# A hybrid decoder step on one Trainium2 core: token norms on two engines, another order for the compressed blocks, other buffers and queues for output weights

## The chip, the cores and the metric

The kernel runs on one core of one Trainium2 chip. The metric is the device time of one execution, in microseconds (us), as the median over several runs. TensorE (PE) multiplies; VectorE (DVE), ScalarE (ACT) and GpSimd (POOL) work element by element; SyncE (SP) issues most of the transfers from memory. Each engine works through its own queue in order.

## The reference, cut to what matters

One layer for a prompt of 1024 tokens and for 8 sequences of 4 new tokens (32 sample rows) with 1024 cached tokens each. `D` is 1024.

```python
h = rms_norm(x, g_pre)              # x * rsqrt(mean(x*x) + eps) * g_pre
u = h @ w_in                        # q, k/v and gates of two head groups, one matrix
# group 1 (8 heads): attention over compressed blocks, selected blocks and a window, mixed by gates
# compressed blocks: 32 rows at stride 16, + cmp_pos, @ w_cmp1, silu, @ w_cmp2, for keys and values,
#   of the prompt's own rows and of the cached rows of each of the 8 sequences
# group 2 (8 heads, "fox"): softmax attention with a forget gate
mix = concat(o_nsa * silu(z_nsa), o_fox * silu(z_fox))
x = x + rms_norm(mix @ w_out, g_post)
y = x + (p @ w_pproj) * sigmoid(x @ w_pgate)
```

## The kernel before

All is written in float32. A matrix product that has to be exact is made of three products of reduced float32 numbers: `split` (L80 to L86) writes a rounded high half on ScalarE and the rest as a low half on VectorE or GpSimd, and the matmuls take high by high, high by low, low by high. The author writes program order; a scheduler, which simulates all engines' timelines, orders each engine's queue from it, places tiles into the buffers of pools and sets all waits. A tile with `bufs=n` gets one of n buffers as soon as one is free; a pool that is opened where another was closed waits for that one's tiles.

**Stages.** First the token norm: nine tiles of x (eight of 128 prompt rows, one of 32 sample rows) are loaded on SP's queue, `sumsq` squares and sums them in two halves on ScalarE (L176), `rstd_of` (L97) makes the factors for four tiles at a time with small VectorE operations and one square root on ScalarE, VectorE and GpSimd scale the tiles (L204, L206), TensorE transposes them (L210), and `split` with the norm vector `gpre` as its scale writes the eight tiles `ht` (L85, L86), which hold the normalized prompt and sample rows transposed, as a high and a low half. `gpre` is loaded behind the x tiles.

Then the projections. `proj` (L227) loads 128 columns of `w_in` in four pieces `wr`, splits them into `wh` (ScalarE) and `wl` (GpSimd), and multiplies in three thirds of 352 columns, 24 matmuls each (L243). In the first part `cmp_proj(e)` makes the rows that are compressed (`cT`; e is 0 for keys, 1 for values). `cmp_pages` loads cached rows of two sequences (16 pieces on SP), and `cmp_chunk` transposes and splits these (L454, L462), multiplies with the compression weights (`w1`, L469) and stores the blocks; `cmp_chunk((NB,), None)` does it for the prompt's own rows from `cT`. `nsa_projections(1)` makes one projection for a later stage, and `gates_and_sums` is a generator whose `next` emits gate and forget sums in pieces. L535 to L578 give their order.

The middle (fox heads, sample attention, attention of group 1) is left alone by the change. At the end `weights` (L1285) loads `w_out` in eight pieces of 128 rows through two `stg` buffers and splits them into the 16 buffers `fwo`, the low halves in turn on VectorE and GpSimd; then, for each of eight prompt tiles, the mix and the gate z are loaded (into the same two `stg` buffers), multiplied, split, multiplied with `w_out` (`mm3`, L1305, 48 matmuls), and `tail` (L1333) norms, adds x and stores. After tile 1 all eight pieces of `w_pgate` are loaded on ScalarE's queue and split. The sample rows follow (`mm_s`, L1314), then the gated part.

Of the kernel before, what the change touches and what calls it, by code (L numbers as in the profile page):

```python
# [27 lines left out]
NB = 8  # L28
# [16 lines left out]
def tile_hymba_step(ctx: ExitStack, tc: tile.TileContext, I: dict, O: dict):  # L45
# [24 lines left out]

    cst = cpool.tile([128, C_ALL], F32, name="cst")
# [88 lines left out]
    HT = [hpool.tile([128, 2, TA], F32R, name=f"ht{k}", tag="ht") for k in range(KD)]  # L160
# [12 lines left out]
    def sumsq(ss, x, n):  # L173
        for c in range(2):
            jk = mm_tile("pt")
            nc.scalar.activation(jk[:n], x[:, c * 512:(c + 1) * 512], AF.Square, accum_out=ss[:, c])  # L176
# [12 lines left out]
    gpre = cpool.tile([128, KD], F32, name="gpre")  # L189
    nc.sync.dma_start(gpre, I["g_pre"][0].rearrange("(k p) -> p k", p=128))  # L190

    for g0 in (0, 4):
        ss = xpool.tile([128, 2, 4], F32, name="ss", bufs=2)
        rs = xpool.tile([128, 4], F32, name="rs", bufs=2)
        xts = []
        for t in range(4):
            xt = xta[g0 + t]
            sumsq(ss[:, :, t:t + 1], xt, 128)
            xts.append(xt)
        nc.vector.tensor_add(ss[:, 0], ss[:, 0], ss[:, 1])  # L200
        rstd_of(xpool, rs, ss[:, 0], 128)
        for t in range(4):
            if t % 2:
                nc.gpsimd.tensor_scalar(xts[t], xts[t], rs[:, t:t + 1], 0.0, op0=OP.mult, op1=OP.add)  # L204
            else:
                nc.vector.tensor_scalar(xts[t], xts[t], rs[:, t:t + 1], None, op0=OP.mult)  # L206
        for k in range(KD):
            ps = mm_tile(("fl", "sc")[k % 2])
# [4 lines left out]
    xs = xta[NT]  # L213
    ss1 = xpool.tile([NS, 2, 1], F32, name="ss1")
    rs1 = xpool.tile([NS, 1], F32, name="rs1")
    sumsq(ss1, xs, NS)
    nc.vector.tensor_add(ss1[:, 0], ss1[:, 0], ss1[:, 1])
    rstd_of(xpool, rs1, ss1[:, 0], NS)
    nc.vector.tensor_scalar(xs, xs, rs1, None, op0=OP.mult)
    ps = mm_tile()  # L220
    for k in range(KD):
        nc.tensor.transpose(ps[:, k * NS:(k + 1) * NS], xs[:, k * 128:(k + 1) * 128], ident[:NS, :NS])
    for k in range(KD):
        split(HT[k][:, 0, T:TA], HT[k][:, 1, T:TA], ps[:, k * NS:(k + 1) * NS], gpre[:, k:k + 1])
# [309 lines left out]

    pgs = cmp_pages((0, 1))  # L535
    cmp_proj(0)
# [18 lines left out]
    G = gates_and_sums()  # L555
    next(G)
    cmp_chunk((0, 1), pgs)
    nsa_projections(1)
    pgs = cmp_pages((2, 3))
    cmp_proj(1)  # L560
    cmp_chunk((2, 3), pgs)
    nsa_projections(1)
    pgs = cmp_pages((4, 5))
    next(G)
    nsa_projections(1)
    next(G)
    cmp_chunk((4, 5), pgs)
    nsa_projections(1)
    next(G)
    pgs = cmp_pages((6, 7))  # L570
    cmp_chunk((NB,), None)
# [713 lines left out]
    def weights(src, nk, pools, stage, q=nc.sync):  # L1285
        w = []
        for k in range(nk):
            wr = stage(k)
            q.dma_start(wr, src[k * 128:(k + 1) * 128])
            p, tag, bufs = pools[k]  # L1290
            h = p.tile([128, D], F32R, name="fwh", tag=tag, bufs=bufs)
            l = p.tile([128, D], F32R, name="fwl", tag=tag, bufs=bufs)
            split(h, l, wr, l_eng=(nc.vector, nc.gpsimd)[k % 2])
            w.append((h, l))
        return w

# [24 lines left out]
    wo = weights(w_out, 8, [(fr, "fwo", 16)] * 8, lambda k: stage())  # L1321
# [33 lines left out]
    nc.sync.dma_start(gpost, raw(I["g_post"], 0, [[0, 128], [1, D]]))  # L1355
    for t in range(NT):
        ts_ = slice(t * 128, (t + 1) * 128)
        mr = stage().rearrange("p (k c) -> p k c", c=128)
        nc.sync.dma_start(mr, d_mix[t // 4][:, :, t % 4 * 128:t % 4 * 128 + 128].rearrange("k p c -> p k c"))
        zr = stage().rearrange("p (k c) -> p k c", c=128)  # L1360
# [157 lines left out]
```

## Time and profile before

| | |
|---|---|
| median of 3 runs | 1294.2 us (1292.38 to 1298.24) |
| profiled execution, own time | 1289.5 us |
| its span, first to last instruction | 1287.7 us |
| mean granted clock of TensorE, 1 is 2.4 GHz | 0.978 |
| TensorE busy (matmuls) | 1194.4 us |
| VectorE / ScalarE / GpSimd busy | 670.0 / 604.1 / 312.8 us |
| read / written in HBM | 128.30 / 36.38 MB |

The profile is one execution; its times are microseconds from the span's start. A matmul's end is modelled, so the distance between two starts tells its pace. In brackets behind an instruction stands how long its engine had been idle before it, and what released it.

### The profile page before, as it was taken

How to read it: one execution, taken by the hardware profiler on the slowest of the kernel's cores; microseconds unless marked ns; L12 is line 12 of the kernel's file. 1: busy time of each engine (PE TensorE's matmuls, PEld its weight loads, DVE VectorE, ACT ScalarE, POOL GpSimd, SP SyncE). 2: the span in 40 equal slices, each digit the busy share in tenths (PEclk: the TensorE clock that was granted, in tenths of full speed). 3: DMA queues.
4: the chain of work that ended last, by engine and by line, in shares of the span. 5: the costliest groups of instructions: out<-in, count | busy, mean ns of one | idle time of the engine just before them, and what ended most of it. 6: DMA issues, size and time to landing. Idle time of an engine off the chain costs nothing. (4 is left out here: it accounts for less than half of the span.)

```text
span 1287.7 us, 23713 instructions
## 1 busy us (share of the span) xinstructions
PE 1194.4 (93%) x8106; PEld 981.2 (76%) x8106; DVE 670.0 (52%) x2062; ACT 604.1 (47%) x1415; POOL 312.8 (24%) x433
## 2 busy tenths in 40 slices
PE   3899989999999999999888899999999798999998
PEld 3798979989899898898865666564664576877776
DVE  4614455335655565553475677575455746443222
ACT  6724453244544555543465676574465742231121
POOL 2510100232222221312222232222112523131212
PEclk8999989999999999999988999999999998999999
DMA  7534311337321313224452543436645475532221
GB/s 243 137 93 136 83 48 49 96 90 227 90 55 48 106 53 95 68 76 149 136 159 95 161 132 127 153 124 223 193 138 174 140 240 171 165 139 82 71 74 38
DMA packets 142731, 157.04 MB, mean 122 GB/s; under 512 B 16586, under 2 KB 109546, under 8 KB 142418
## 3 DMA queue, kind: packets, MB, share of 16 engines
q1 hardware_dynamic: 141378, 151.06, 38.1%
q10 hardware_dynamic: 1152, 4.19, 0.9%
q8 instruction: 64, 1.05, 0.3%
q14 instruction: 57, 0.47, 0.1%
q0 software_dynamic: 80, 0.26, 0.1%
HBM read 128.30 MB, written 36.38 MB: 128 GB/s over the span
## 5 line engine op out<-in xcount | busy, mean ns | idle before, releaser
L243 PE MATMUL ps_fl<-ht,wh 128*128 128x352 f32 x1440 | 368.0, 329 | 5.6 <-DVE os L511 3.7
L243 PEld LDWEIGHTS ps_fl<-ht,wh 128*128 128x128 f32 x1440 | 256.6, 191 | 10.5 <-DVE os L511 4.0
L243 PE MATMUL ps_fl<-ht,wl 128*128 128x352 f32 x720 | 236.7, 329 | 0.0
L641 ACT ACTIVATE s<-s,m 128x64 f32<-128x64 f32 (+8 forms) x256 | 164.5, 644 | 59.6 <-DVE m L639 56.6
L83 POOL TENSOR_TENSOR wl<-wr,wh 128x256 fp32r<-128x256 f32 x120 | 89.1, 748 | 261.1 <-ACT wh L82 258.1
L644 POOL TENSOR_SCALAR s<-s,rs 128x64 f32<-128x64 f32 (+8 forms) x160 | 93.1, 601 | 234.6 <-DVE rs L1002 129.1
L243 PEld LDWEIGHTS ps_fl<-ht,wl 128*128 128x128 f32 x720 | 137.0, 190 | 1.1 <-issue 0.4
L633 PE MATMUL ps_sc<-kh,q 128*128 128x320 f32 (+12 forms) x304 | 117.3, 390 | 16.7 <-DVE m L639 10.7
L659 PE MATMUL ps_pt<-cst,s 128*128 128x128 f32 x816 | 127.0, 282 | 2.6 <-ACT s L93 1.0
L639 DVE CUSTOM_DVE_ANT_0 s<-ps_sc,bias 128x128 f32<-128x128 f32 (+10 forms) x224 | 80.4, 389 | 79.4 <-PE ps_pv L703 23.5
L659 PEld LDWEIGHTS ps_pt<-cst,s 128*128 128x128 f32 x816 | 97.1, 143 | 22.0 <-issue 5.6
L93 ACT ACTIVATE s<-ps_pt 128x512 f32<-128x512 f32 (+2 forms) x164 | 86.3, 538 | 56.3 <-PE ps_pt L659 44.6
L634 PE MATMUL ps_sc<-kl,q 128*128 128x320 f32 (+12 forms) x304 | 101.3, 336 | 1.5 <-DVE kl L622 1.5
L633 PEld LDWEIGHTS ps_sc<-kh,q 128*128 128x128 f32 x304 | 58.5, 192 | 50.5 <-DVE m L639 17.6
L639 DVE CUSTOM_DVE_ANT_0 s<-ps_sc,bias,m 128x320 f32<-128x320 f32 (+10 forms) x168 | 87.1, 523 | 7.0 <-PE ps_sc L634 3.4
L82 ACT CAST wh<-wr 128x256 fp32r<-128x256 f32 x120 | 47.7, 404 | 68.5 <-PE ps_fl L243 40.5
L95 DVE COPY s<-ps_pt 128x512 f32<-128x512 f32 (+2 forms) x84 | 49.8, 593 | 36.9 <-PE ps_pt L659 34.2
L769 POOL TENSOR_TENSOR mc<-bias,cst 128x128 f32<-128x128 f32 x64 | 30.2, 476 | 148.7 <-DVE m L639 134.7
L634 PEld LDWEIGHTS ps_sc<-kl,q 128*128 128x128 f32 x304 | 59.0, 194 | 3.7 <-DVE kl L622 1.7
L647 DVE TENSOR_SCALAR s<-s,rs 128x128 f32<-128x128 f32 (+7 forms) x96 | 54.5, 595 | 1.9
L1305 PE MATMUL ps_sc<-fwh,xh 128*128 128x512 f32 x128 | 50.8, 397 | 2.1 <-ACT xh L82 2.1
L1305 PE MATMUL ps_sc<-fwl,xh 128*128 128x512 f32 x128 | 50.1, 391 | 0.0
(444 smaller groups left out, 2191.1 us busy)
## 6 DMA issues: line engine op xcount, KB each, us to landing
kp<-in_cache_fox_kv_dram SPq DMA_DIRECT2D x64, 256.0 KB
vp<-in_cache_fox_kv_dram SPq DMA_DIRECT2D x64, 256.0 KB
wr<-in_w_in_dram SPq DMA_DIRECT2D x120, 128.0 KB
pg<-in_cache_cmp_kv_dram SPq DMA_DIRECT2D x64, 128.0 KB
pg<-in_cache_slc_kv_dram SPq DMA_DIRECT2D x64, 128.0 KB
d_g<-d_r SPq DMA_DIRECT2D x1, 4800.0 KB
bias<-d_g SPq DMA_DIRECT2D x8, 520.0 KB
X<-in_x_prompt_dram SPq DMA_DIRECT2D x8, 512.0 KB
```

The source lines that it names most:

```text
L83: (l_eng or nc.vector).tensor_tensor(l, src, h.bitcast(F32), op=OP.subtract)
L93: nc.scalar.activation(out, in_, AF.Copy, scale=1.0 if scale is None else scale)
L95: nc.vector.tensor_copy(out, in_)
L243: nc.tensor.matmul(ps[:, :CH], lhsT=w[k // 2][:, k % 2], rhs=HT[k][:, hl, s], start=n == 0, stop=n == 3 * KD - 1)
L633: nc.tensor.matmul(out, lhsT=qi, rhs=ks[0][:, k0:k0 + n], start=True, stop=False)
L634: nc.tensor.matmul(out, lhsT=qi, rhs=ks[1][:, k0:k0 + n], start=False, stop=True)
L639: nc.vector.tensor_tensor_reduce(o, p, bi, scale=-1.0, scalar=BIG if x == 0 else m, op0=OP.add, op1=OP.min, accum_out=m)
L641: nc.scalar.activation(s_ap, s_ap, AF.Exp, scale=-1.0, bias=m, accum_out=ssum)
L644: nc.gpsimd.tensor_scalar(s_ap, s_ap, r, 0.0, op0=OP.mult, op1=OP.add)
L647: nc.vector.tensor_scalar(s_ap, s_ap, r, None, op0=OP.mult)
L659: nc.tensor.transpose(ps[:, (2 * x + a) * 128:(2 * x + a + 1) * 128], S[:, a, (b0 + x) * 128:(b0 + x + 1) * 128], ident)
L1305: nc.tensor.matmul(o, lhsT=a[al][:, k], rhs=w[k][wl][:, c * 512:(c + 1) * 512], start=k == 0 and x == 0, stop=k == nk - 1 and x == 2)
```

## The change

`gpre` is loaded ahead of all else. The eight tiles `ht` become one tile of eight parts. The square of a whole tile is one instruction, on ScalarE for even and on VectorE for odd tiles, and writes its product into a part of the new tile that isn't in use yet; a square root of a constant stands ahead of them. The sample rows' factor is made with that of the second four tiles; the scaling is spread over three engines. The sample rows are multiplied by `gpre` and split in one piece. Both `cmp_proj` and the first `next(G)` go ahead of the pages and compression weights; the prompt's own chunk goes ahead of those of the sequences; and a projection stands ahead of every chunk. Six of the eight raw pieces of `w_out` are loaded into `fwo` buffers, the low halves of all these weights go to VectorE, z is loaded ahead of the mix, and the pieces of `w_pgate` come in pairs after tiles 1 to 4, on SP's queue.

```diff
--- before.py
+++ after.py
@@ -68,6 +68,8 @@
     def mm_tile(tag="fl"):
         return pst[1].tile([128, 512], F32, name="ps_" + tag, tag=tag, bufs=pst[2][tag])
 
+    gpre = cpool.tile([128, KD], F32, name="gpre")
+    nc.sync.dma_start(gpre, I["g_pre"][0].rearrange("(k p) -> p k", p=128))
     cst = cpool.tile([128, C_ALL], F32, name="cst")
     nc.sync.dma_start(cst, I["cst"])
     ident = cst[:, CO["ID"]]
@@ -157,7 +159,8 @@
     hpool = rst.enter_context(tc.tile_pool(name="hpool", bufs=8, side="right", reuse_waits="tile"))
     wpool = rst.enter_context(tc.tile_pool(name="wpool", bufs=3, side="right", reuse_waits="tile"))
 
-    HT = [hpool.tile([128, 2, TA], F32R, name=f"ht{k}", tag="ht") for k in range(KD)]
+    HA = hpool.tile([128, KD, 2, TA], F32R, name="ht", bufs=1)
+    HT = [HA[:, k] for k in range(KD)]
 
 
     qst = ExitStack()
@@ -170,10 +173,8 @@
     def xtile():
         return cp_.tile([128, 8 * XW], F32, name="X", tag="X", bufs=4)
 
-    def sumsq(ss, x, n):
-        for c in range(2):
-            jk = mm_tile("pt")
-            nc.scalar.activation(jk[:n], x[:, c * 512:(c + 1) * 512], AF.Square, accum_out=ss[:, c])
+    warm = cpool.tile([128, 1], F32, name="warm")
+    nc.scalar.activation(warm, ones[:, 0:1], AF.Sqrt)
 
     xta = []
     for t in range(NT + 1):
@@ -186,42 +187,56 @@
             xt = x2[:, (t % 2) * D:(t % 2 + 1) * D]
             nc.sync.dma_start(xt, x_p[t * 128:(t + 1) * 128, :])
         xta.append(xt)
-    gpre = cpool.tile([128, KD], F32, name="gpre")
-    nc.sync.dma_start(gpre, I["g_pre"][0].rearrange("(k p) -> p k", p=128))
-
+
+    def sumsq(ss, x, n, t):
+
+        jk = HA[:, 7 - t % 4].rearrange("p h c -> p (h c)")
+        if t % 2:
+            nc.vector.scalar_tensor_tensor(jk[:n, :D], x, 1.0, x, op0=OP.mult, op1=OP.mult, accum_out=ss)
+        else:
+            nc.scalar.activation(jk[:n, :D], x, AF.Square, accum_out=ss)
+
+    def scale(x, r, eng):
+        if eng == 0:
+            nc.vector.tensor_scalar(x, x, r, None, op0=OP.mult)
+        elif eng == 1:
+            nc.scalar.activation(x, x, AF.Identity, scale=r)
+        else:
+            nc.gpsimd.tensor_scalar(x, x, r, 0.0, op0=OP.mult, op1=OP.add)
+
+    rss = []
     for g0 in (0, 4):
-        ss = xpool.tile([128, 2, 4], F32, name="ss", bufs=2)
-        rs = xpool.tile([128, 4], F32, name="rs", bufs=2)
-        xts = []
+        ss = xpool.tile([128, 5], F32, name="ss", bufs=2)
+        rs = xpool.tile([128, 5], F32, name="rs", bufs=2)
+        rss.append(rs)
+        nc.gpsimd.memset(ss, float(D))
         for t in range(4):
-            xt = xta[g0 + t]
-            sumsq(ss[:, :, t:t + 1], xt, 128)
-            xts.append(xt)
-        nc.vector.tensor_add(ss[:, 0], ss[:, 0], ss[:, 1])
-        rstd_of(xpool, rs, ss[:, 0], 128)
-        for t in range(4):
-            if t % 2:
-                nc.gpsimd.tensor_scalar(xts[t], xts[t], rs[:, t:t + 1], 0.0, op0=OP.mult, op1=OP.add)
-            else:
-                nc.vector.tensor_scalar(xts[t], xts[t], rs[:, t:t + 1], None, op0=OP.mult)
+            sumsq(ss[:, t:t + 1], xta[g0 + t], 128, t)
+        if g0:
+            sumsq(ss[:NS, 4:5], xta[NT], NS, 0)
+        rstd_of(xpool, rs, ss, 128)
+        if g0 == 0:
+            for t in range(4):
+                scale(xta[t], rs[:, t:t + 1], t % 2)
+    for g0 in (0, 4):
+        xts = xta[g0:g0 + 4]
+        if g0:
+            for t in range(4):
+                scale(xts[t], rss[1][:, t:t + 1], (0, 2, 1, 2)[t])
+            scale(xta[NT], rss[1][:NS, 4:5], 0)
         for k in range(KD):
-            ps = mm_tile(("fl", "sc")[k % 2])
+            ps = mm_tile(("pt", "sc")[k % 2])
             for t in range(4):
                 nc.tensor.transpose(ps[:, t * 128:(t + 1) * 128], xts[t][:, k * 128:(k + 1) * 128], ident)
             s = slice(g0 * 128, g0 * 128 + 512)
             split(HT[k][:, 0, s], HT[k][:, 1, s], ps, gpre[:, k:k + 1])
-    xs = xta[NT]
-    ss1 = xpool.tile([NS, 2, 1], F32, name="ss1")
-    rs1 = xpool.tile([NS, 1], F32, name="rs1")
-    sumsq(ss1, xs, NS)
-    nc.vector.tensor_add(ss1[:, 0], ss1[:, 0], ss1[:, 1])
-    rstd_of(xpool, rs1, ss1[:, 0], NS)
-    nc.vector.tensor_scalar(xs, xs, rs1, None, op0=OP.mult)
     ps = mm_tile()
     for k in range(KD):
-        nc.tensor.transpose(ps[:, k * NS:(k + 1) * NS], xs[:, k * 128:(k + 1) * 128], ident[:NS, :NS])
-    for k in range(KD):
-        split(HT[k][:, 0, T:TA], HT[k][:, 1, T:TA], ps[:, k * NS:(k + 1) * NS], gpre[:, k:k + 1])
+        nc.tensor.transpose(ps[:, k * NS:(k + 1) * NS], xta[NT][:, k * 128:(k + 1) * 128], ident[:NS, :NS])
+    xsT = xpool.tile([128, KD, NS], F32, name="pc", tag="th", bufs=2)
+    nc.vector.tensor_tensor(xsT, ps[:, :KD * NS].rearrange("p (k c) -> p k c", c=NS),
+                            gpre[:, :, None].to_broadcast([128, KD, NS]), op=OP.mult)
+    split(HA[:, :, 0, T:TA], HA[:, :, 1, T:TA], xsT)
 
 
     def proj(c0, ev):
@@ -532,8 +547,11 @@
             f(c0, u)
         del nsa_out[:n]
 
+    cmp_proj(0)
+    cmp_proj(1)
+    G = gates_and_sums()
+    next(G)
     pgs = cmp_pages((0, 1))
-    cmp_proj(0)
     w1, w2, pos = [], [], []
     for e in range(2):
         w1h = cp_.tile([128, 16, 128], F32R, name="w1h", bufs=2)
@@ -552,23 +570,20 @@
         pT = cp_.tile([128, 16], F32, name="posT", bufs=2)
         nc.vector.tensor_copy(pT, ps[:, :16])
         pos.append(pT.rearrange("p (u j) -> p j u", u=2))
-    G = gates_and_sums()
+    nsa_projections(1)
+    cmp_chunk((NB,), None)
+    nsa_projections(1)
+    cmp_chunk((0, 1), pgs)
+    pgs = cmp_pages((2, 3))
     next(G)
-    cmp_chunk((0, 1), pgs)
     nsa_projections(1)
-    pgs = cmp_pages((2, 3))
-    cmp_proj(1)
     cmp_chunk((2, 3), pgs)
-    nsa_projections(1)
     pgs = cmp_pages((4, 5))
     next(G)
     nsa_projections(1)
+    cmp_chunk((4, 5), pgs)
+    pgs = cmp_pages((6, 7))
     next(G)
-    cmp_chunk((4, 5), pgs)
-    nsa_projections(1)
-    next(G)
-    pgs = cmp_pages((6, 7))
-    cmp_chunk((NB,), None)
     nsa_projections(1)
     next(G)
     cmp_chunk((6, 7), pgs)
@@ -1282,17 +1297,21 @@
     def stage_x(k):
         return fp.tile([128, 1280], F32, name="wx", tag=("xh", "xl")[k % 2], bufs=2)[:, :D]
 
-    def weights(src, nk, pools, stage, q=nc.sync):
+    def weights(src, ks, pools, stage):
         w = []
-        for k in range(nk):
+        for k in ks:
             wr = stage(k)
-            q.dma_start(wr, src[k * 128:(k + 1) * 128])
+            nc.sync.dma_start(wr, src[k * 128:(k + 1) * 128])
             p, tag, bufs = pools[k]
             h = p.tile([128, D], F32R, name="fwh", tag=tag, bufs=bufs)
             l = p.tile([128, D], F32R, name="fwl", tag=tag, bufs=bufs)
-            split(h, l, wr, l_eng=(nc.vector, nc.gpsimd)[k % 2])
+            split(h, l, wr)
             w.append((h, l))
         return w
+
+    def stage_o(k):
+
+        return fr.tile([128, D], F32, name="wro", tag="fwo", bufs=16) if k < 6 else stage()
 
     def halves(x):
         return [x[:, 0:512], x[:, 512:1024]]
@@ -1318,7 +1337,7 @@
             nc.scalar.copy(o, full[c][32:64])
             nc.vector.tensor_tensor(o, o, full[c][0:32], op=OP.add)
 
-    wo = weights(w_out, 8, [(fr, "fwo", 16)] * 8, lambda k: stage())
+    wo = weights(w_out, range(8), [(fr, "fwo", 16)] * 8, stage_o)
     ast.close()
     fpa = fst.enter_context(tc.tile_pool(name="fpa", bufs=1, reuse_waits="tile"))
     fp = fst.enter_context(tc.tile_pool(name="fp", bufs=1, reuse_waits="tile"))
@@ -1353,12 +1372,13 @@
 
     gpost = fr.tile([128, D], F32, name="gpost")
     nc.sync.dma_start(gpost, raw(I["g_post"], 0, [[0, 128], [1, D]]))
+    wg_ = []
     for t in range(NT):
         ts_ = slice(t * 128, (t + 1) * 128)
+        zr = stage().rearrange("p (k c) -> p k c", c=128)
+        nc.sync.dma_start(zr, d_z[:, :, ts_].rearrange("k p c -> p k c"))
         mr = stage().rearrange("p (k c) -> p k c", c=128)
         nc.sync.dma_start(mr, d_mix[t // 4][:, :, t % 4 * 128:t % 4 * 128 + 128].rearrange("k p c -> p k c"))
-        zr = stage().rearrange("p (k c) -> p k c", c=128)
-        nc.sync.dma_start(zr, d_z[:, :, ts_].rearrange("k p c -> p k c"))
         nc.vector.tensor_tensor(mr, mr, zr, op=OP.mult)
         mp = (fr, fp)[t % 2]
         mh = mp.tile([128, 8, 128], F32R, name="mh", tag="mh")
@@ -1369,8 +1389,8 @@
         o = [mm_tile(("fl", "sc")[t % 2]) for _ in range(2)]
         mm3(o, (mh, ml), wo, 8, (0, 1))
         tail(o, xr, 128, t)
-        if t == 1:
-            wg_ = weights(w_pgate, 8, [(fpa, "fwa", 8)] * 4 + [(fp, "fwb", 8)] * 4, stage_x, nc.scalar)
+        if 1 <= t <= 4:
+            wg_ += weights(w_pgate, (2 * t - 2, 2 * t - 1), [(fpa, "fwa", 8)] * 4 + [(fp, "fwb", 8)] * 4, stage_x)
     a_s = rows32(8)
     split(a_s[:, :8, 0:32], a_s[:, :8, 32:64], mixs)
     xr = row_tile()
@@ -1379,7 +1399,7 @@
     mm_s(o[:NS], a_s, wo, 8)
     tail(halves(o[:NS]), xr[:NS], NS, NT)
 
-    wp = weights(w_pproj, 2, [(fr, "fwo", 16)] * 2, lambda k: stage())
+    wp = weights(w_pproj, range(2), [(fr, "fwo", 16)] * 2, lambda k: stage())
 
     def gated(y, x1, n, g, pj):
```

## Rows read from the trace of the kernel before

**Rows 1.** The page, parts 1 and 2: busy time of all engines, TensorE's slices.
```profile
PE 1194.4 (93%) x8106; PEld 981.2 (76%) x8106; DVE 670.0 (52%) x2062; ACT 604.1 (47%) x1415; POOL 312.8 (24%) x433
...
PE   3899989999999999999888899999999798999998
```

**Rows 2.** Busy time by window: start:end, length, each engine, PEclk, DMA share, GB/s.
```profile
20.00:40.00 20.00, 14.24 (x77) 10.39 (x75) 17.28 (x35) 15.43 (x31) 9.78 (x11) 0.81 0.63 160
```

**Rows 3.** Timeline of SP's queue (start, us, engine, line, op, tiles), first 30 us.
```profile
7.94 0.39 SPq L190 DMA_DIRECT2D gpre<-in_g_pre_dram  x1
11.42 14.92 SPq L148 DMA_DIRECT2D pg<-in_cache_cmp_kv_dram  x16
26.39 1.61 SPq L231 DMA_DIRECT2D wr<-in_w_in_dram  x3
28.04 1.72 SPq L543 DMA_DIRECT2D w1r<-in_w_cmp_dram  x2
```

**Rows 4.** Timeline of TensorE, first projection and some page transposes.
```profile
40.19 0.63 PE L243 MATMUL ps_fl<-ht,wh 128*128 128x352 f32 x1 [0.33 <-DVE ht L86]
...
49.91 1.04 PE L454 MATMUL ps_sc<-cst,pg 128*128 128x128 f32 x8
...
54.32 0.32 PE L243 MATMUL ps_fl<-ht,wl 128*128 128x352 f32 x1
54.48 0.32 PE L243 MATMUL ps_fl<-ht,wh 128*128 128x352 f32 x1
```

**Rows 5.** Groups by line, 0 to 330 us: busy us, mean ns | idle before.
```profile
L82 ACT CAST X<-cT 64x512 fp32r<-64x512 f32 x8 | 8.6, 1071 | 0.1
L83 DVE TENSOR_TENSOR X<-cT,X 64x512 fp32r<-64x512 f32 x8 | 8.2, 1022 | 1.1 <-ACT X L82 0.7
L86 DVE SCALAR_TENSOR_TENSOR ht<-ps_sc,gpre,ht 128x512 fp32r<-128x512 f32 x8 | 5.9, 743 | 2.1 <-ACT ht L85 2.1
...
L204 POOL TENSOR_SCALAR X<-X,rs 128x1024 f32<-128x1024 f32 x4 | 5.3, 1344 | 19.9 <-DVE rs L106 15.2 <-ACT ht L85 4.7
```

**Rows 6.** Timeline of VectorE, 10 to 17 us.
```profile
12.12 0.17 DVE L100 TENSOR_SCALAR rs_v<-ss 128x4 f32<-128x4 f32 x1
...
14.68 0.16 DVE L103 TENSOR_TENSOR rs_a<-rs 128x4 f32<-128x4 f32 x1 [2.17 <-ACT rs L102]
...
15.47 2.29 DVE L206 TENSOR_SCALAR X<-X,rs 128x1024 f32<-128x1024 f32 x2
```

**Rows 7.** Busy time by window around 170 us, columns as in rows 2.
```profile
160.00:180.00 20.00, 14.04 (x89) 12.82 (x88) 15.56 (x39) 13.73 (x20) 2.85 (x4) 0.81 0.27 71
175.00:180.00 5.00, 4.68 (x23) 3.75 (x23) 4.20 (x13) 1.24 (x3) 2.22 (x4) 0.50 0.59 161
180.00:185.00 5.00, 5.00 (x29) 5.00 (x28) 0.55 (x2) 0.00 (x0) 0.00 (x0) 0.74 0.10 24
```

**Rows 8.** Timelines of VectorE, GpSimd and TensorE, last attention tile.
```profile
1027.95 1.59 DVE L1000 TENSOR_SCALAR rs<-sums 128x6 f32<-128x6 f32 x1 [1.20 <-ACT s L641]
...
1027.17 2.34 POOL L83 TENSOR_TENSOR fwl<-stg,fwh 128x1024 fp32r<-128x1024 f32 x1 [5.89 <-ACT fwh L82]
...
1032.26 0.33 PE L686 MATMUL ps_pt<-cst,s 128*128 128x128 f32 x1 [4.71 <-POOL s L644]
```

**Rows 9.** Timelines of TensorE, VectorE and GpSimd after the second output tile.
```profile
1063.71 0.39 PE L1305 MATMUL ps_sc<-fwl,mh 128*128 128x512 f32 x1
1063.94 0.40 PE L1305 MATMUL ps_sc<-fwh,ml 128*128 128x512 f32 x1
1070.70 0.79 PE L1314 MATMUL ps_pv<-fwh,as 128*128 128x512 f32 x1 [6.37 <-DVE as L83]
...
1077.34 0.39 PE L1305 MATMUL ps_fl<-fwh,mh 128*128 128x512 f32 x1
...
1068.03 2.29 DVE L106 TENSOR_TENSOR r<-r,rs_a 128x1 f32<-128x1 f32 x1
...
1064.67 5.62 POOL L83 TENSOR_TENSOR fwl<-wx,fwh 128x1024 fp32r<-128x1024 f32 x2 [5.70 <-ACT fwh L82]
```

## What was predicted

> **What bounds the kernel now.** I read the page's first two parts first [rows 1]. TensorE's matmuls are busy for 93% of the span, VectorE for 52%, ScalarE for 47%. The forty slices show where the other 7% lies: in the first two slices, the sixth, four from the twentieth on (attention, which the change leaves alone), the thirty-second, the thirty-fourth and the last. Since TensorE is nearly full elsewhere, whatever starts its stream earlier or closes a gap should move the end by as much. So I looked at the gaps alone, in order of time: the instructions of TensorE and of the other engines around each of them, the queue of SP, and windows of some microseconds.
>
> The front. In the stretch from 20 to 40 us TensorE shows 14.24 us of transposes at a granted clock of 0.81, VectorE 17.28 and ScalarE 15.43 [rows 2]: here the vector engines set the pace. The first projection matmul starts at 40.19, the last of that projection at 54.48 [rows 4]; the matmuls follow each other 0.16 us apart when nothing is in the way. Three things stand ahead of it. The factors of the first four token tiles come late: the chain stands still for 2.17 us between reciprocal and square root, behind the squares and a table load in ScalarE's queue, and scaling begins at 15.47 [rows 6]. The page loads of the first two sequences hold SP's queue from 11.42 for 14.92 us, so the first projection weights are issued at 26.39 [rows 3]. And the splits of those pages are mixed among the 16 splits of the normalized prompt, which cost VectorE 743 ns each [rows 5].
>
> The second gap is in the window from 160 to 180: TensorE has 14.04 us busy of 20, and afterwards runs five microseconds at the lower level, 1.2 GHz (granted clock 0.50), and then at a mean of 0.74 [rows 7]. What fills ScalarE and VectorE there is the compression of the prompt itself, 8 casts of 1071 ns and 8 subtractions of 1022 ns [rows 5].
>
> The third is at the end of attention. TensorE waits 4.71 us, until 1032.26, for GpSimd's scaling; the reciprocal chain ahead of that began with an operation over 6 columns that took 1.59 us, while GpSimd computed a low half of the output weights, from 1027.17 for 2.34 us [rows 8]. An operation of the same kind over 4 columns took 0.17 us [rows 6]. The fourth: the second output tile ends at about 1064.2, then nothing for 6.37 us, then the sample rows' 16 matmuls until 1077.34 [rows 9]. VectorE was late there: a multiplication of one column took 2.29 us, beside two low halves of gate weights on GpSimd that took 5.62 us in all [rows 9]. The third output tile needs the PSUM that the first tile's norm, queued on VectorE, still holds.
>
> **The change part by part.** *Norm.* Squares: 8 tiles on ScalarE become 4 there and 4 on VectorE; the square root's table is loaded at the start. That removes the 2.17 us stall and some waiting behind squares, so I let scaling start at 14.0 instead of 15.47 (the first four tiles still have to be loaded). The norm vector's transfer moves ahead of everything on SP: its issue takes 0.39 us [rows 3] and delays the tiles by about that; I take 0.5 (bounds 0.4 and 1.5). From 14.0 VectorE has: four scalings at 1.15 (2.29 for two [rows 6]), 4.6; two squares, at twice the 743 ns of half as wide an operation [rows 5], an estimate, 3.0; six small operations at 0.17 [rows 6], 1.0; 16 splits at 0.743, 11.9. Together 20.5, so all of the prompt is split at about 34.5. The sample rows, once 8 pairs of small splits, are one pair.
>
> *Order.* Both compressed projections, then the gate loads, then the pages. The projection weights thus go out behind the prompt, past the 16 page loads, and are there before 20 us. The first third of a projection needs only the first half of the prompt and runs while the second half is split. The second third ends as the splits do, and the last third is 24 matmuls at 0.16, 3.9 us. So the first projection ends near 39 instead of 54.6: 15.6 us. By then TensorE had also done the 32 page transposes of the first chunk, which now come later; 8 take 1.04 us [rows 4], so 4.2 go off. Front: 11 us. Lower bound 4 (a wait for the whole normalized tile, below), upper 14 (scalings at half that price, and part of the second projection fitted in).
>
> What becomes late: pages and the compression weights. They are loaded in pieces through two buffers, the first from 28.04 on [rows 3], and are now wanted at about 39 plus two projections of 11.5 (72 matmuls at 0.16), so there is room. GpSimd's queue has the projection weights' low halves and two scalings of 1344 ns [rows 5] beside these, and nothing of it is on the path unless they come late.
>
> *Prompt's blocks first, a projection per chunk.* The 8.6 and 8.2 us of splits [rows 5] now stand beside two whole projections of 11.5 us each, and each chunk's page splits beside one. The gap is 6.0 us of idle time (20 less 14.04). The clock cost half of 4.68 us, 2.3, and a quarter of 5, 1.3 [rows 7]: 9.6 in all. The order of the queues is new, and small waits will come up; I take 8 (bounds 3 and 9.6).
>
> *Output weights.* Six raw tiles get buffers of their own, so loads no longer wait for the splits two tiles back, and the low halves leave GpSimd for VectorE. The 1.59 us operation should fall to 0.17: 1.4 us gained. Against it, VectorE gets four more subtractions, in a stretch where it is fairly full; cost unknown, between nothing (in its gaps) and 5.9 us (an estimate: four times twice the 743 ns of an operation half as wide [rows 5]); I take 1, nearer to nothing, since the weights are wanted only after attention.
>
> *Gate weights.* Eight loads after tile 1 become two after each of tiles 1 to 4, on SP's queue, all halves on VectorE. GpSimd no longer holds VectorE up, and a tile has 11 us of matmuls (48 at 0.23) for two splits. I expect the third tile straight behind the second: 6.4 us of idle time. The sample's 16 matmuls, 6.64 us from 1070.70 to 1077.34 [rows 9], would be 16 times the 0.23 us between two starts before the gap [rows 9], 3.7: 2.9 more. Together 9.3, I take 9 (bounds 2, and 13, if tile 0's matmuls also fill part of the 4.71 us wait). Behind a waiting weight load on SP would stand the next tile's inputs and the stores of this one.
>
> Sum: 11 + 8 + 1.4 + 9, less 0.5 and 1: 28 us. The profiled execution took 1289.5 us, its span 1287.7; less 28 that is 1261.5. The median of the runs lies 4.7 above the profiled one, so 1266.
>
> One rule speaks against the front. The Trainium skill, "SBUF — State Buffer", section "Who interferes with whom", says that VectorE and GpSimd share a port pair, so that a VectorE operation with two SBUF inputs, or in a two-port mode, and a GpSimd operation that reads SBUF exclude each other for a whole instruction. The new squares on VectorE have two SBUF inputs. By the rule each of GpSimd's two scalings could hold VectorE up in full, and the sum would be 25 instead of 28; the 1.15 us scalings that I used already hold part of that.
>
> **The rivals.**
> (1) *Whole-tile wait.* The eight normalized tiles become one. If a projection waits for the whole of it, its first matmul starts at 34.5 and it ends at 46.0: the front gives 4 instead of 11, 1273. For it: the trace can't show such a tile. Against: in this kernel token tiles already share one buffer by halves and are scaled one by one.
> (2) *The first stage is held by its feeders.* The compression weights come behind 16 page loads that take SP 14.92 us [rows 3]. If the prompt's chunk finds them some 13 us late, TensorE waits at its head, and the two gains of 19 shrink to 6: 1279.
> (3) *The gap after tile 1 stays.* The tail's small operations may still queue behind a split that waits for its load. Then the 9 are gone: 1275.
> (4) *Port exclusion in full*, as computed from rows: two GpSimd scalings of 1.34 us: 3 us less, 1269.
> (5) *Slower.* On SP's queue a weight load that waits for a staging buffer stops the inputs of the next tile. If each of the four tiles then shows a gap like the old one, 9.3 us, that is 37 in place of 9.3, on top of the front's gain: 28 - 9 - 28 = -9, so 1303. It decides from some 7 us in each of four tiles on. Against it: a tile lasts 11 us, and a weight piece is only 512 KB, as much as one token tile.
>
> **How the numbers follow.** The forecast has 0.55, rivals (1) 0.12, (2) 0.13, (3) 0.08, (4) 0.06, (5) 0.06. The predicted time is the forecast's, 1266. The range has to take in (1) to (4) with some overlap among them, and on the low side the upper bounds of front and gate weights (14 and 13 instead of 11 and 9, with all of the second gap): 1254 to 1283. Under 0.5%, 6.5 us, a measurement can't tell a difference; faster means under 1287.7. Two of the rivals at once come near that line, and (5) lies beyond: faster 0.87, same 0.06, slower 0.07.
>
> **What would show it.** Right: first projection matmul near 20 us, end of that projection near 39; no window of 5 us between 40 and 230 with TensorE under 4 us busy; the stage's last instructions about 19 us earlier than before; no gap between the second and third output tile; no VectorE operation of a few columns over 1 us near the end of attention. Wrong: a first projection matmul after 30 us; a wait of TensorE for compression weights; SP waiting between two output tiles; a longer attention part, which the sum takes as unchanged.

## The result and the profile after

The kernel after takes 1302.7 us (median of 7 runs, 1301.13 to 1306.79) beside 1294.2 for the kernel before (7 runs, 1287.41 to 1298.24): ratio 1.0076, 95% interval 1.0051 to 1.01. It is slower by 0.8%; 1266 was predicted, with a chance of 0.07 for slower. The profiled execution took 1301.71 us, its span 1299.9, 12.2 longer than before.

The first reading is where TensorE comes later. These are starts of its instructions in the two timelines, in us:

| place | before | after | difference |
|---|---|---|---|
| first projection matmul | 40.19 | 35.05 | -5.1 |
| end of the first stage (first matmul with the compressed values `vcp`) | 234.7 | 249.8 | +15.1 |
| first output matmul | 1041.90 | 1058.15 | +16.2 |
| first product of the gated part | 1150.1 | 1162.7 | +12.6 |

So the first stage, from which 19 us were to come, lost 15, though its first projection starts 5 earlier; the end won some 4, and attention between them lost 1. TensorE has the same work, 1195.5 us beside 1194.4, in a longer span.

The windows (columns as in [rows 2]) place it. From 20 to 40 TensorE has 10.15 us busy where it had 14.24, at a mean clock of 0.66; the losses go on to 100. The gap of [rows 7] is nearly closed: 18.71 of 20. First the kernel after, then three windows of the kernel before:

```profile
20.00:40.00 20.00, 10.15 (x52) 8.37 (x50) 11.53 (x20) 10.13 (x21) 12.56 (x12) 0.66 0.40 109
40.00:60.00 20.00, 15.47 (x100) 14.43 (x98) 10.66 (x16) 14.46 (x24) 7.88 (x8) 0.88 0.32 90
60.00:80.00 20.00, 14.88 (x85) 14.02 (x84) 5.87 (x10) 7.57 (x13) 2.93 (x4) 0.84 0.26 67
80.00:100.00 20.00, 16.92 (x92) 15.27 (x91) 7.50 (x18) 8.20 (x15) 0.00 (x0) 0.76 0.43 126
160.00:180.00 20.00, 18.71 (x126) 18.33 (x127) 13.02 (x40) 10.44 (x20) 0.00 (x0) 0.91 0.38 105
```

```profile
40.00:60.00 20.00, 18.54 (x115) 17.52 (x116) 11.87 (x26) 14.69 (x35) 10.09 (x10) 0.93 0.45 123
60.00:80.00 20.00, 19.92 (x146) 19.02 (x145) 3.56 (x18) 4.03 (x9) 0.00 (x0) 1.00 0.42 122
80.00:100.00 20.00, 18.95 (x126) 18.50 (x125) 5.48 (x10) 8.98 (x19) 5.89 (x8) 1.00 0.30 84
```

TensorE's timeline names the waits:

```profile
30.11 1.12 PE L230 MATMUL ps_pt<-cst,X 128*128 128x128 f32 x4 [6.60 <-DVE ht L88]
...
35.05 0.66 PE L258 MATMUL ps_fl<-ht,wh 128*128 128x352 f32 x1
...
57.50 0.64 PE L277 MATMUL ps_fl<-cst,cT 128*32 128x128 f32 x2 [4.14 <-ACT nat L95]
...
75.11 0.23 PE L569 MATMUL ps_fl<-cst,pn 16*128 16x16 f32 x1 [1.70 <-DVE sn L278]
78.63 0.58 PE L489 MATMUL ps_pv<-X,w1h 128*128 128x260 f32 x1 [3.29 <-DVE X L85]
```

Each is followed to its head on another engine. The 6.60 end with a split of `ht` on VectorE, which waited for ScalarE, which waited for a transfer. ScalarE's timeline and SP's queue (the one of [rows 3]):

```profile
27.21 0.62 ACT L84 CAST w1h<-w1r 128x512 fp32r<-128x512 f32 x1 [5.29 <-DMA w1r<-in_w_cmp_dram]
27.74 0.20 ACT L104 ACTIVATE rs<-rs_a 128x5 f32<-128x5 f32 x1
27.84 0.67 ACT L87 ACTIVATE ht<-ps_pt,gpre 128x512 fp32r<-128x512 f32 x1
```

```profile
16.00 2.93 SPq L285 DMA_DIRECT2D bf<-in_b_fgate_dram  x1
24.45 0.92 SPq L561 DMA_DIRECT2D w1r<-in_w_cmp_dram  x2
...
78.27 8.95 SPq L150 DMA_DIRECT2D pg<-in_cache_cmp_kv_dram  x14
```

The cast of the first compression weights stands in ScalarE's queue ahead of the second half's square root and of 14 splits, and those weights are issued only at 24.45. From 18.93 to 24.45 SP shows no transfer: in its instruction list stand there the readings of 16 page numbers, two sequences of eight, into registers (L146), called by `cmp_pages`, which program order has ahead of the weights. The pages themselves go out from 72.7 on, since their buffers are still taken. (The expectations of e5 and e9 below speak of 32 numbers; the list has 16.)

VectorE (as in [rows 6]): the stall before the square root's result fell from 2.17 to 0.90 us, but tiles came later and a square of 1.22 us went between the factor's small operations, so scaling starts at 16.17, not 14.0. The last split of `ht` is at 49.58, not 34.5, and the first projection ends near 51.9, not 39.

```profile
14.34 0.17 DVE L105 TENSOR_TENSOR rs_a<-rs 128x5 f32<-128x5 f32 x1 [0.90 <-ACT rs L104]
14.42 1.22 DVE L195 SCALAR_TENSOR_TENSOR ht<-X 128x1024 fp32r<-128x1024 f32 x1
...
16.17 1.42 DVE L201 TENSOR_SCALAR X<-X,rs 128x1024 f32<-128x1024 f32 x2
...
49.58 0.75 DVE L88 SCALAR_TENSOR_TENSOR ht<-ps_sc,gpre,ht 128x512 fp32r<-128x512 f32 x1 [1.59 <-ACT ht L87]
```

At the end (timelines of VectorE, GpSimd and TensorE, as in [rows 8, 9]) the slow operation over 6 columns is down from 1.59 to 0.17 us as forecast, yet TensorE's wait for GpSimd grew from 4.71 to 7.33. The gap ahead of the sample rows is 3.21 instead of 6.37.

```profile
1044.22 0.17 DVE L1015 TENSOR_SCALAR rs<-sums 128x6 f32<-128x6 f32 x1
...
1045.00 5.66 POOL L659 TENSOR_SCALAR s<-s,rs 128x64 f32<-128x64 f32 x5 [11.26 <-DVE rs L1017]
...
1040.63 0.39 PE L718 MATMUL ps_pv<-s,vcz 128*64 128x128 f32 x4
1040.95 0.41 PE L648 MATMUL ps_sc<-kh,q 128*128 128x320 f32 x1
1041.20 0.31 PE L649 MATMUL ps_sc<-kl,q 128*128 128x320 f32 x1
1048.85 0.48 PE L701 MATMUL ps_pt<-cst,s 128*128 128x128 f32 x1 [7.33 <-POOL s L659]
...
1083.72 0.79 PE L1333 MATMUL ps_pv<-fwh,as 128*128 128x512 f32 x1 [3.21 <-DVE as L85]
```

Before, the second of the last pair of score matmuls stood at 1024.27, ahead of 3 us of weighted sums; now the pair stands behind them. The kernel before:

```profile
1024.27 0.31 PE L634 MATMUL ps_sc<-kl,q 128*128 128x320 f32 x1
1024.51 1.08 PE L697 MATMUL ps_pv<-s,VW 128*64 128x256 f32 x8
...
1027.15 0.39 PE L703 MATMUL ps_pv<-s,vcz 128*64 128x128 f32 x4
```

From that matmul to the one that needs the scaled result it took 8.0 us before (to 1032.26 [rows 8]) and 7.7 after. GpSimd's five scalings in it became slower, 5.66 us instead of 3.70, but the distance as a whole did not grow: the wait is longer because the 3 us of cover are gone.

### The profile page after: what moved, and what is told of

Same layout as the page of the kernel before. It is cut to its first block, busy times and chain, and to the rows that moved or that the text cites. A ratio compares the mean times of both kernels' runs of the same rounds, so it can differ in the third digit from the quotient of the medians.

```text
span 1299.9 us, 23670 instructions
## 1 busy us (share of the span) xinstructions
PE 1195.5 (92%) x8106; PEld 984.8 (76%) x8106; DVE 674.9 (52%) x2063; ACT 599.8 (46%) x1384; POOL 293.0 (23%) x424
## 5 line engine op out<-in xcount | busy, mean ns | idle before, releaser
L258 PEld LDWEIGHTS ps_fl<-ht,wh 128*128 128x128 f32 x1440 | 259.2, 193 | 8.6 <-DVE os L526 4.1
L659 POOL TENSOR_SCALAR s<-s,rs 128x64 f32<-128x64 f32 (+8 forms) x160 | 96.5, 624 | 250.8 <-DVE rs L1017 132.8
```

Of the source, the lines that this page charges most:

```text
L258: nc.tensor.matmul(ps[:, :CH], lhsT=w[k // 2][:, k % 2], rhs=HT[k][:, hl, s], start=n == 0, stop=n == 3 * KD - 1)
L659: nc.gpsimd.tensor_scalar(s_ap, s_ap, r, 0.0, op0=OP.mult, op1=OP.add)
```

## The experiments

Ratios are to the kernel before on the same chip, with their 95% intervals.

### Which part loses

e1, e2, e3 and e4 are made by putting whole parts of the diff on the kernel before: the norm; the order; both; the end. No code is new.

Norm alone. 

> The kernel before with the norm part alone (factors first, squares and scalings on two engines, one tile for the normalized prompt, the norm vector loaded first). Theory: the first stage was lost by the new order of its queues, not by the norm, so this one takes about 1292 (1288 to 1296), and the stage's last matmuls end within 4 us of the 234.7 of before. Rival: the norm itself costs (tiles land 1.2 us later, one tile for all): 1300 or more, the stage's end at 242 or later.

Measured: 1290.78 us, 0.9989 (0.9967 to 1.0012); the first stage ends at 233.5. As the theory had it.

Order alone. 

> The kernel before with the order part alone (both compressed projections, gate loads, then pages; prompt's blocks first; a projection per chunk). Theory: here lies the loss, about 15 us: 1309 (1303 to 1314), the stage's end near 250. Rival, the norm is to blame: within 4 us of 1294. Second rival, only both together lose: within 4 us of 1294 here and in the run with the norm alone.

Measured: 1308.61 us, 1.0134 (1.01 to 1.0168); the stage ends at 245.3, and TensorE has the same kind of wait as in after, 6.16 us until 31.52. The order is the loss, without any help of the norm.

Both, without the end. 

> The kernel after with the end of before: norm and order changed, output and gate weights as they were. Theory: the end part won some 4 us, so this is 4 slower than after: 1307 (1304 to 1310). Rival, the end is worth nothing (its gain at the gap eaten by the longer wait for GpSimd): 1303.

Measured: 1305.44 us, 1.0106 (1.0075 to 1.0138); the stage ends at 249.3. Between this and after lie 0.3%, which the intervals don't separate from nothing.

The end alone. 

> The kernel before with the end part alone (raw output weights in their ring, gate weights in pairs, all low halves on VectorE). Theory: 4 us faster, 1290 (1287 to 1292): the gap ahead of the sample rows' matmuls falls from 6.4 to some 3 us, the wait for GpSimd after the last attention tile grows from 4.7 to some 7. Rival, no gain: 1294. Second rival, the forecast's 9 us come once the first stage no longer shifts the attention part: 1285.

Measured: 1291.99 us, 0.9989 (0.9964 to 1.0014): no gain that the runs can tell from none, where the theory had 4 us. The wait for GpSimd is 7.33 us again, the gap 3.8 instead of 6.4: one pays for the other.

### What in the order loses

The page numbers:

```diff
 cmp_proj(0); cmp_proj(1); G = gates_and_sums(); next(G)
-pgs = cmp_pages((0, 1))
 w1, w2, pos = [], [], []
 for e in range(2):
     ...
     pos.append(pT.rearrange("p (u j) -> p j u", u=2))
+pgs = cmp_pages((0, 1))
```

> The kernel after, with the page loads of the first two sequences called behind the block of compression weights instead of ahead of it; on SP's queue the 32 page numbers are then read (18.9 to 24.4 us in after) behind the first compression weights. Theory: these weights are issued near 19 instead of 24.45 and land near 22, ScalarE no longer stands 5.29 us before their cast with the second half's square root and splits behind it, the first projection matmul comes near 30 instead of 35.05: some 5 us, and up to 2 more of clock: 1297 (1295 to 1299). Rival: another wait at the same place takes over (the fourth piece of the projection weights is now behind the page numbers): 1302.

Measured: 1294.79 us, 1.0004 (0.9979 to 1.0028), so 0.7% below after, a little more than the theory said. ScalarE's wait before the weights' cast is 0.78 us, and the first projection matmul comes at 29.5. The rival has a part: SP issues nothing from 21.4 to 27.0, where the numbers are now read, and the wait for the next piece of projection weights is new:

```profile
22.58 0.62 ACT L84 CAST w1h<-w1r 128x512 fp32r<-128x512 f32 x1 [0.78 <-DMA w1r<-in_w_cmp_dram]
...
29.27 0.40 ACT L84 CAST wh<-wr 128x256 fp32r<-128x256 f32 x1 [4.31 <-DMA wr<-in_w_in_dram]
```

The position tables (`cmp_pos`, 16 columns each):

```diff
+pos = []
+for e in range(2):
+    pn = ...; nc.sync.dma_start(pn, ...); transpose; copy; pos.append(...)
 cmp_proj(0)
 cmp_proj(1)
 ...
-    pn = ...        # the same lines, behind the compression weights
```

> The kernel after, with the two small position tables loaded, transposed and copied ahead of the compressed projections instead of behind the compression weights. Theory: ahead of the prompt's blocks TensorE waits 1.70 and 3.29 us for a 16-column table that stands on VectorE and ScalarE behind the 8.5 us split of the second projection; with the table there the blocks start near 73.5 instead of 78.6, and at a higher clock: 5 to 7 us, 1297 (1295 to 1299). Rival: the page loads (landing up to 88 us) then bound this stretch, and the gain is under 2 us: 1301.

Measured: 1293.17 us, 0.9998 (0.9971 to 1.0024), 0.8% below after. The waits of 1.70 and 3.29 us are gone and the prompt's blocks start at 72.0 instead of 78.6, more than the theory said. The wait at 30 us stays (5.3).

> Both of the former edits in one kernel. Theory: two separate waits, so the gains add up: 1291 (1288 to 1294), near the kernel before. Rival: what one closes the other opens again: 1297, no better than the better of the two.

Measured: 1289.89 us, 0.9956 (0.9942 to 0.997). After lies at 1.0076; the two edits alone took 0.0072 and 0.0078 off, together 0.0120. So they add up for the most part, and two small blocks put elsewhere undo the whole loss. (The end part, still in this kernel, has no share in it that the runs show: e4.)

The prompt's blocks last, as before (`cmp_chunk((NB,), None)` put straight ahead of the last chunk of pages, all else as in after; in the kernel before a projection and a `next(G)` stood between the two). 

> The kernel after, with the prompt's compressed blocks in their former place, before the last chunk of pages, and everything else as it is in after. Theory: the loss lies at the queues' heads in the first 90 us, and without the prompt's blocks there the first chunk of pages, loaded from 72.7 on, is waited for instead: 1303 to 1308. Rival: taking the prompt's blocks first is the loss: 1294 or less.

Measured: 1309.09 us, 1.0122 (1.0075 to 1.0169). So the prompt's blocks in front are not the loss. The waits of TensorE in the first 252 us (total, times, longest) show what comes with this order: the late pages, and for `os`, at 203 us, a wait of the kind that ended the old gap of [rows 7]:

```profile
PE ps_pt L230 <- DVE ht L88: 7.7, 2, 6.1
PE ps_sc L469 <- DMA pg<-in_cache_cmp_kv_dram: 7.2, 6, 4.2
PE ps_fl L258 <- DVE os L526: 5.9, 1, 5.9
```

The page numbers behind the last load of compression weights on SP:

```diff
+if hold and len(page_dmas) < 16:       # hold: the last w1r load
+    with tc.issue_after(hold[0]):
+        issue()
-if len(page_dmas) >= 16:
+elif len(page_dmas) >= 16:
```

> The two edits together (pages behind the weights, position tables early), and the reading of the 32 page numbers put behind the last of the compression weights on SP's queue, where it holds nothing up (the pages themselves go out from 73 us on in any case). Theory: with both edits ScalarE still stands 3.95 us before a piece of projection weights that is issued at 26.5, behind the page numbers; this wait goes too: 3 to 4 us, 1286 (1284 to 1288). Rival: TensorE waits at that place for the second half's factors anyway: 1290.

Measured: 1289.27 us, 0.9976 (0.9956 to 0.9996). This is e7 with one thing more. ScalarE's wait for that piece of projection weights is gone (TensorE's, for splits, fell from 4.9 to 1.8) and the first stage ends at 232.9 instead of 236.4, but the time is that of e7; theory had 3 to 4 us, and the rival's number came. In the profiled execution 2.7 of the 3.5 us are left at the first output matmul and 1.8 at the end; the runs can't tell them from none.

With both queue heads free, this kernel shows what is left of the forecast. The first projection starts at 31.5 and ends near 47.7, not 39, and the last split of `ht` starts at 45.10, not before 34.5. ScalarE's half of the splits now waits for TensorE: the second half's tiles are scaled by 29.4 us, but their transposes stand among the projection's matmuls, from 36.3 on (timelines of ScalarE and VectorE):

```profile
36.57 0.69 ACT L87 ACTIVATE ht<-ps_pt,gpre 128x512 fp32r<-128x512 f32 x1 [4.51 <-PE ps_pt L234]
...
45.10 0.74 DVE L88 SCALAR_TENSOR_TENSOR ht<-ps_sc,gpre,ht 128x512 fp32r<-128x512 f32 x1
```

In its first stage TensorE is idle for 31.7 us, in that of before for 30.6 (after: 43.3). The old waits are gone, the 5.6 us that ended the gap of [rows 7] and 3.5 for page transfers, but new ones stand in their place: 4.1 us for a copy (`nat`), 3.7 for low halves of the compressed rows (`X`), 2.4 for the sample rows (`xs`).

The longest of these, the 4.1 us at 53 us for `nat`, is for a copy that stands behind half of the prompt's casts of [rows 5]. On top of e9:

```diff
-    naturals(cT, 0, t0, nat)
+    naturals(cT, 0, t0, nat, nc.vector.tensor_copy)   # both copies on VectorE
```

> The kernel with page numbers late and position tables early, and the four copies of the compressed projections' natural layout on VectorE instead of in turn on both engines. Theory: TensorE's wait of 4.1 us at 53 us for a copy that stands on ScalarE behind 4.3 us of the prompt's casts is gone, and with it some us at the lower clock: 4 to 6 us below 1289, 1284 (1282 to 1287). Rival: VectorE's copies stand behind its own subtractions, or the pages bound what follows: 1288.

Measured: 1296.34 us, 1.0023 (1.0003 to 1.0043): 0.5% (6 us) above e9 by the ratios, against both theory and rival. The wait went (0.3 and 1.2 us stay), and the first stage ends at 230.3, the best of all. But the last projection of the middle part is now done at 635.1 instead of 644.0, and from there TensorE has less to do. Windows of e9 and then of this kernel:

```profile
600.00:650.00 50.00, 42.56 (x272) 38.65 (x270) 22.58 (x88) 17.88 (x50) 10.84 (x23) 0.93 0.48 163
```

```profile
600.00:650.00 50.00, 35.94 (x216) 32.12 (x218) 21.26 (x92) 15.91 (x45) 8.68 (x19) 0.83 0.57 196
```

The gain was given back, with interest, around 640, where projections had filled TensorE's waits for the vector engines. That the missing projections are the cause is argued from these rows, not shown by a run of its own.

### The end, in its parts

The gate weights alone, on the kernel before:

```diff
-if t == 1:
-    wg_ = weights(w_pgate, 8, ..., stage_x, nc.scalar)
+if 1 <= t <= 4:
+    wg_ += weights(w_pgate, (2 * t - 2, 2 * t - 1), ..., stage_x)   # low halves on VectorE
```

> The kernel before with the gate weights alone changed (loaded in pairs after output tiles 1 to 4 on SP's queue, their low halves on VectorE); output weights as before. Theory: the gain of the end part is here, some 3 us of the gap ahead of the sample rows' matmuls; the wait of 4.7 us for GpSimd after the last attention tile stays: 1291 (1289 to 1292). Rival, the forecast: 9 us, 1285.

Measured: 1287.11 us, 0.9953 (0.9924 to 0.9982), between theory and forecast. The gap ahead of the sample rows is 1.73 us, at a higher clock, and from the first output matmul to the first product of the gated part it takes 101.4 us (1045.8 to 1147.2), where before took 108.2: 6.8 us.

```profile
1069.93 0.50 PE L1314 MATMUL ps_pv<-fwh,as 128*128 128x512 f32 x1 [1.73 <-DVE as L83]
```

The output weights alone (raw tiles for k < 6 from the ring `fwo`; all low halves on VectorE). 

> The kernel before with the output weights alone changed (six raw tiles in their ring, all low halves on VectorE); gate weights as before. Theory: this is the losing half of the end part, the first output matmul comes 3 to 4 us later than the 1041.9 of before, of which the gap after the second tile takes some back: 1297 (1295 to 1298). Rival, the forecast: 0.4 us gained, 1294; second rival, the longer wait for GpSimd comes from the gate weights: 1294 as well.

Measured: 1300.12 us, 1.0046 (1.0026 to 1.0067), worse than expected: the wait for GpSimd is 7.33 us and the gap ahead of the sample rows 10.3. Its TensorE timeline has the last score matmuls behind the weighted sums, as after has:

```profile
1030.22 0.39 PE L703 MATMUL ps_pv<-s,vcz 128*64 128x128 f32 x4
1030.54 0.41 PE L633 MATMUL ps_sc<-kh,q 128*128 128x320 f32 x1
1038.43 0.48 PE L686 MATMUL ps_pt<-cst,s 128*128 128x128 f32 x1 [7.33 <-POOL s L644]
```

All low halves on VectorE without the raw ring, with the gate weights in pairs (`l_eng=nc.vector`). 

> The kernel before with the gate weights in pairs, and all low halves of the output weights on VectorE, but no raw ring. Theory: the low halves on VectorE cost, since they stand beside GpSimd's last scaling (5.66 us beside two of them in after, 3.70 in before) and ahead of the sums' reciprocals: the wait for GpSimd is 7 us again, 1290 (1288 to 1292), 3 more than with the gate weights alone. Rival: the raw ring is what costs, and this one takes 1287 with a wait of some 4.9 us.

Measured: 1289.28 us, 0.9971 (0.995 to 0.9992). The time doesn't separate it from e10. The wait does: 4.53 us, with the scores ahead of the weighted sums. The long wait goes with the raw ring (7.33 in e4, e11 and after; 4.5 to 5.0 in e10, e12, e14 and e16; 1.12 in e15, also without a ring). So does what is left of the gap ahead of the sample rows: 3.0 to 3.9 us with ring and gate pairs (after, e4 to e7, e9, e13), 1.7 to 1.9 in e10, e12 and e14, none here, with all halves on VectorE. The theory that the halves make the wait long falls; that they cost nothing isn't shown, since from the last scores to the scaled result it takes 9.9 us here beside 8.0 in before. Why the ring makes the scheduler turn the order of TensorE's queue isn't shown either. The loading of z ahead of the mix never ran alone; e10 and e11 together (0.9953 and 1.0046) give what e4 gives with it, so nothing is left for it that the runs could show.

### Putting it together

Mended order and gate weights, no ring. 

> The kernel after with the page numbers late and the position tables early, and of the end part only the gate weights. Theory: the gains add up: 9 us under before by the front, order and gate weights together, 1283 (1281 to 1286). Rival, without the ring the loads of the output weights wait for splits and the end gives nothing: 1287.

Measured: 1285.48 us, 0.9939 (0.9915 to 0.9963), as theory had it.

The same with the copies on VectorE. 

> Page numbers late, position tables early, natural copies on VectorE, and of the end part the gate weights alone. Theory: 1281 (1278 to 1284), 4 below the run without the copies' change. Rival: 1285, no gain, since the pages' splits bound the stretch up to 150 us.

Measured: 1289.03 us, 0.9968 (0.9948 to 0.9988). No gain, as e13 had shown; by the ratios 0.3% above e12, with intervals that touch.

Norm and gate weights, with the old order and the old output weights. 

> The kernel before with the norm part and the gate weights alone; order and output weights as before. Theory: the two small gains add up, 1286 (1284 to 1289), so the new order, mended, is worth no more than the old one. Rival, the mended order is worth some us of its own: this one is 3 or more slower than the 1285 of the run with the mended order and the gate weights.

Measured: 1282.29 us, 0.9914 (0.9889 to 0.9938), the fastest of all: 0.9% below before and 1.6% below after. It takes none of the new order. Beside the mended order with the same gate weights (e12), the intervals overlap: no gain of the new order is seen, and no loss either. In the window of the output tiles TensorE has 47.69 us busy at full clock; before had 43.63 at 0.90 (first row this kernel, second row before).

```profile
1040.00:1090.00 50.00, 47.69 (x219) 38.15 (x216) 28.95 (x47) 18.63 (x31) 9.06 (x3) 1.00 0.70 232
1040.00:1090.00 50.00, 43.63 (x192) 34.83 (x187) 26.75 (x34) 18.32 (x30) 16.11 (x6) 0.90 0.64 215
```

## Why the prediction was wrong

*The step that failed: "so all of the prompt is split at about 34.5", and with it the front's 11 us.* The sum was made of VectorE's own instructions, as if its queue were the only one. A split is two instructions, and its first half runs on ScalarE, whose queue got the compression weights' cast in its midst; that cast waited for a transfer, the transfer for SP, and SP for page numbers that nobody needed before 72 us. The prediction said of the pages and weights that they "are now wanted at about 39 plus two projections", so late was no matter. They were not wanted earlier, but the instruction that waited for them stood ahead of others that were. e5 shows it: the same instructions, the numbers read later, 0.7% less.

The two heads of queues account for the loss; they don't account for the gain that didn't come. With both free, e9 still has the last split at 45.10, for the step was wrong a second time: the splits also wait for transposes in TensorE's queue, 4.51 us at once in e9, which the sum left out as well. e9's first stage ends at 232.9 us (239.3 in e12's profile), not at the 215.7 that 19 us less would give.

*The transposes booked too low.* The prediction took 4.2 us off the gain for the 32 page transposes that now come later, their bare time on TensorE. In the kernel before 20 of them ran ahead of the first projection matmul, while TensorE waited for the splits, and 12 inside the projection. In after they take the stretch from 84.2 to 92.5, 8.3 us, in which 2.0 us of waits for page transfers and 1.1 for page splits stand. A filler was moved out of a gap into a full stretch.

*Order, 8 us.* The mechanism was right at its own place: idle time from 160 to 180 fell from 6.0 to 1.3 us. But the same casts and subtractions, moved to 52 to 77, took along what had been hidden: the copies behind them (4.14 us) and the position tables (5.0 us), with a granted clock of 0.88 from 40 to 60 and 0.84 from 60 to 80 where before had 0.93 and 1.00. e6 shows the tables' share, 0.8%. That a projection would stand "beside" the prompt's splits was wrong as well: after the second projection TensorE's queue goes straight to the prompt's blocks, and the third projection starts at 92.7. Its last two pieces of weights could be cast only at 68.98 and 69.94, as the second's matmuls released the buffers of `wh`; the scheduler took the blocks first.

*Norm.* Wrong by 2.2 us in the start of scaling, and without effect on the whole: alone it gives 0.9989.

*Output weights, 0.4 us.* The 1.59 us operation fell to 0.17 as worked out; what was missed is that the order of TensorE's own queue would change with the ring and lose 3 us of cover. Measured alone: 0.46% slower, with the gap ahead of the sample rows at 10.3 us instead of 6.37 besides.

*Gate weights, 9 us.* Right in mechanism, mis-sized by little: 6.8 us in e10. In after the output stage takes 104.6 us, so 3.6 are left; the gap stays at 3.21 with the ring, as in every kernel with ring and gate pairs, while without the ring it is under 2 us, also where all halves are on VectorE (e16).

*The rivals.* (1), the whole-tile wait, is refuted: projection matmuls run from 35.05 on, while the splits of the second half are written until 49.58. (2), the stage held by its feeders, was nearest: the compression weights it named were late, but the harm was done on ScalarE's queue at 22 us, not at the chunk's head. (3) came half: 3.21 of 6.37 us. (5) named the right time, 1303, by luck: no gap opened at each output tile. (4) was not put to the test: the squares on VectorE (1.22 us each) were over at 18.75 us and GpSimd's two scalings began at 31.79, 1.6 us each instead of 1.34. The Trainium skill, "SBUF — State Buffer", section "Who interferes with whom", has a VectorE operation with two SBUF inputs contend with a GpSimd operation that reads SBUF. The traces fit this where the two meet: five scalings on GpSimd took 5.66 us beside two subtractions in after, and 3.70 in before; but the longer wait followed the order of the score matmuls, not this.

What stays open: why e9's 3.5 us earlier end of the first stage doesn't reach the end of the kernel, whether e13's loss near 640 us is due to the missing projections alone, how much each of the new waits in e9's first stage is worth, and why the ring turns the order of TensorE's queue.

## What to carry to other kernels

When a block of code is moved, every queue that it touches moves, not only the engine that was to gain: before counting a gain, write down for each engine in order what would stand ahead of the instruction that matters, and what each of those waits for. Small things without a bar in the profile, such as reading page numbers or a 16-column table, can stand at the head of a queue and cost more than the work that was optimized. And work that runs in another engine's wait is free where it is; moved into a full stretch it has a price, and so has a filler that is used up early.

## What the runs showed of the hardware

Reading 16 page numbers into registers on SP took 5.5 us (18.93 to 24.45 in after; 21.4 to 27.0 in e5) in which that queue issued nothing, some 0.34 us each, and no busy time is shown for it. After TensorE's wait of 6.60 us in after, and after that of 5.3 us at the same place in e6, matmuls of the first projection start 0.29 us apart until about 38 us, and 0.16 from then on. In after the granted clock from 35 to 37.5 us is 0.50, the lower level of 1.2 GHz, which fits this pace. In e6 the same column reads 1.00 there, which contradicts it: the column should be read together with the distance between starts. Two profiled executions of the same first stage (e9, e12) ended it at 232.9 and 239.3 us; a single profile is not good for differences of a few microseconds.
